# Seven products for a quarter of the query and key projection in a two-layer trunk kernel

## The chip, the cores and the metric

The kernel runs on one core of one Trainium2 chip. The metric is the device time of one execution in microseconds (us); lower is better. Before the change it is 1020.06 us, the median of three runs (1020.04 to 1020.19). One further execution was profiled; its trace is what the views below are read from.

## The reference

The model has two layers over 256 tokens of width 2048, all in float32. The first mixes HGRN2 and RG-LRU heads; after it and after the second layer, a gate built from the hidden state scales a per-layer embedding. The second layer is an mLSTM. The change touches its first projection, which gives queries and keys, and the hand-over to it from the gate of the first layer:

```python
    h = h + mix
    pl = rmsnorm(p[i].astype(h.dtype) @ ple_w[i], ple_norm[i])
    h = h + jax.nn.sigmoid(h @ ple_gate_w[i]) * pl       # end of layer 0: the gate "g0"
    hn = rmsnorm(h, o_norm[j])                           # layer 1 begins
    u = hn @ o_w_in[j]                                   # 2048 x 8208
    qk = u[..., 0:2 * C_QK]                              # 2048 columns: queries, keys
    v = u[..., o0:o0 + C_WIDTH]                          # 2048 columns: values ("ov")
    qk = jax.nn.silu(causal_conv(qk, c_conv_w[j], c_conv_b[j]))
```

## The kernel before

**Tiling.** A projection of 2048 columns is cut into four chunks of 512 columns. Its contraction of 2048 is cut into four quarters (`kq` 0 to 3) of 512. The 256 tokens are two halves (`hf`) of 128. The stationary side of a matmul is a 128x128 block of features by tokens, the moving side 128x512 of weights. Float32 exactness is kept by splitting both sides into a high and a low part and adding three matmuls (high-high, high-low, low-high). So one quarter of one chunk is 2 halves x 4 blocks x 3 = 24 matmuls (`quarter_tok`, lines 200 to 215, or `plain`, 241 to 247).

**Weights.** A quarter of a chunk comes as two tiles of 128x1024 (512 KB). SyncE (SP) issues the load into one of five `raw` tiles (line 134); ScalarE (ACT) copies the high part into one of four `whi` tiles (137), VectorE (DVE) subtracts for the low part in one of four `wlo` (138). The same split for tiles that are loaded by hand is `split_weights` (217 to 223).

**Seven products.** `seven` (288 to 397) computes two chunks at once for a pair of token halves. In the quarters listed in `kqs` it splits the contraction in two, which makes a 2x2 by 2x2 block product, and does that with seven block products of six matmuls each in place of eight. The weight tiles are X, Y, Z and W; sums of them are formed in place, by DVE (`add`) or by an accumulating transfer that POOL issues (`add_loaded`, line 314, when `acc` is true). The features enter in four combinations that `combos` (249 to 286) makes from the features of the quarter and stores, high and low, in two tiles `q4`. The products go to PSUM banks A, F, B (`mm`) and E (`mx`), partial results to two half tiles `b5` and `g`. The remaining quarters are plain. The order is a string: `a` and `b` are plain quarters of the first and second chunk, the digits are products, `.` lets waiting side work advance, `A` and `F` hand out a result.

**Side work.** Generators wait in named lanes; `pump()` advances each lane by one step, in the middle of a quarter and at `.`. Tile allocation and waits are made by the framework, which also orders the instructions of each engine by priority: the splits of weights come early (`high_priority`, lines 136, 220).

**Around the change.** `two_and_seven` (187 to 198) runs the gate g0: two plain chunks, then `seven` on the other two. `ple_gate` (610 to 626) applies tanh and the embedding, turns each finished chunk into features by a DVE transpose and a hop through device memory that POOL issues (`to_features`, `across`, lines 562 to 588 and 683 to 692), and stores them, scaled and split, as `acth` in twelve `ahl` tiles (lines 142 to 153). Two steps of `acth` are a quarter. `gate_sums` (1148 to 1156) reads the weight tile `wg` for 32 small matmuls.

Queries and keys (1226 to 1241) ran as `chunks`: `project_two` does chunks 0 and 1 in the order (0,0) (0,1) (1,0) (1,1) (0,2) (1,2) (0,3) (1,3) of (chunk, quarter), then chunks 2 and 3 follow whole. Each finished chunk goes through `features` (1196 to 1224): transpose, hop, convolution, SiLU. The lane "combos" (1228 to 1233) made the combinations of quarter 0 ten steps into this stage, in `h` tiles, for the value projection that comes next (`value_halves`, 1377 to 1384).

Of the kernel before, what the change touches and what calls it, by code (L numbers as in the profile page):

```python
# [19 lines left out]
P = 128  # L20
# [5 lines left out]
ORDERS = {1: "a5a6.2aA7b.4F.bb", 2: "a5.2aA64.7F.bb"}  # L26
LATE = "a526.a7b4aAF.bb"
# [18 lines left out]
def trunk(ctx: ExitStack, tc: tile.TileContext, a, out):  # L46
# [116 lines left out]
    def project_tok(w, j, act, before=None, begun=None):  # L163

        ps = begun or [pm.tile([P, 512], F32, name="mm", tag="mm") for _ in range(2)]
        for kq in range(1 if begun else 0, 4):
            if before is not None:
                before(kq)
            quarter_tok(w, j, kq, act, ps)
        return ps  # L170
# [77 lines left out]

    def combos(act, kq, qs, pool, tag, bufs=None, offset=0):
# [14 lines left out]
        def keep(c, names):  # L264
            q = pool.tile([P, 1024], F32R, name="q4", tag=tag, bufs=bufs)
            with tc.high_priority(offset=offset):
                s.copy(q[:, 0:512], c)
                v.tensor_tensor(out=q[:, 512:1024], in0=c, in1=q[:, 0:512].bitcast(F32), op=ALU.subtract)
            for n, name in enumerate(names):
                qs[name, kq] = [[q[:, i * 512 + n * T + k * P:i * 512 + n * T + (k + 1) * P] for k in range(2)]  # L270
                                for i in range(2)]
# [16 lines left out]
    def seven(w, j, act, qs, kqs, room, part, home=None, order=None, acc=None, before=None, third=None):  # L288
# [38 lines left out]
        def combo(n):  # L327
            return [[t for kq in kqs for t in qs[n, kq][x]] for x in range(2)]
# [5 lines left out]
        A, F, B = (pm.tile([P, 512], F32, name="mm", tag="mm") for _ in range(3))  # L334
# [12 lines left out]
        if third is not None:  # L347
            plain(w, j + 2, kqs[0], act, third, (True, True))
        Y = load(room, 1, 1)
        product(E, combo(4), split(Y), home is None)  # L350
        W = X
        if not acc:
            W = load(ring, 1, 0)
            add(Y, W)
            add(W, X)
        did = set()
        for op in order or ORDERS[len(kqs)]:
            if op in "ab":
# [251 lines left out]
    def ple_gate(hq, parts, pls, rp, hss, gain, lane, more):  # L610

        nxt = {}
# [13 lines left out]
        return nxt  # L626
# [513 lines left out]
    wt = e0.tile([P, KT, 32], F32, name="wg")  # L1140
# [17 lines left out]
    acth = ple_gate(hq, two_and_seven(a["g0"], act, ready(act, "fe"), (e0, "q4", 2), in_e0), pls, rp0, hss0, "on", "fg", gate_sums)  # L1158
# [34 lines left out]
    with tc.tile_pool(name="m1", bufs=2) as m1:  # L1193
# [32 lines left out]
        qs = {}  # L1226

        def early():
            for _ in range(10):
                yield  # L1230
            yield from combos(acth, 0, qs, hp, "h")

        start("combos", early())
        for j, ps in enumerate(chunks(a["oqk"], 4, acth, ready(acth, "fg"))):
            if j == 0:
                drain("norm")
            t = m1.tile([P, 2, 512], F32, name="tqk", tag="vt", bufs=6)
            for hf in range(2):
                s.activation(t[:, hf], ps[hf], AF.Copy, scale=norm["rt"][:, hf:hf + 1])
            start(f"qk{j}", features(t, j))  # L1240
            step(f"qk{j}")
# [7 lines left out]
        li, xf, ab, Bc, Mx = (t8(n) for n in ("li", "xf", "ab", "Bc", "Mx"))  # L1249
        lf = xf  # L1250
# [126 lines left out]
        def value_halves():  # L1377
# [3 lines left out]
            drain("combos", "spill")  # L1381
# [153 lines left out]
        def gates():  # L1535
# [3 lines left out]
            for hf, ps in enumerate(project_tok(a["g1"], 2, act, None, third)):  # L1539
                yield 2, hf, ps  # L1540
# [196 lines left out]
```

## Time and profile before

| what | value |
|---|---|
| median of 3 runs | 1020.06 us |
| profiled execution, its own time | 1020.23 us |
| its span, first to last instruction | 1018.4 us |
| mean granted TensorE clock | 0.998 |
| matmuls / VectorE / ScalarE instructions | 5158 / 1234 / 949 |
| gate g0, `seven` part | 429.4 to 473.1 us |
| queries and keys | from 472.9 us |

How to read it: PE is the matmul part of TensorE and PEld its loading of stationary blocks, which overlaps; DVE is VectorE, ACT ScalarE, POOL GpSimd, SP SyncE. L235 is line 235 of the kernel before. A matmul group `mm<-whi,ahl` writes a PSUM tile `mm` from `whi` and `ahl`. In the views, "idle before" is the time in which an engine had nothing to do, with what ended it behind the arrow.

### The profile page before, as it was taken

How to read it: one execution, taken by the hardware profiler on the slowest of the kernel's cores; microseconds unless marked ns; L12 is line 12 of the kernel's file. 1: busy time of each engine (PE TensorE's matmuls, PEld its weight loads, DVE VectorE, ACT ScalarE, POOL GpSimd, SP SyncE). 2: the span in 40 equal slices, each digit the busy share in tenths (PEclk: the TensorE clock that was granted, in tenths of full speed). 3: DMA queues.
4: the chain of work that ended last, by engine and by line, in shares of the span. 5: the costliest groups of instructions: out<-in, count | busy, mean ns of one | idle time of the engine just before them, and what ended most of it. 6: DMA issues, size and time to landing. Idle time of an engine off the chain costs nothing.

```text
span 1018.4 us, 14515 instructions
## 1 busy us (share of the span) xinstructions
PE 1009.4 (99%) x5158; PEld 838.1 (82%) x5158; DVE 842.8 (83%) x1234; ACT 661.4 (65%) x949; POOL 101.3 (10%) x182
## 2 busy tenths in 40 slices
PE   9999999999999999999999999999999999999996
PEld 8888888888888888888888888888888888888886
DVE  7858969969687887898669997888889997999794
ACT  7675554686875554666557877776676777466562
POOL 0111101011111112021011100000011110102000
PEclk9999999999999999999999999999999999999999
DMA  9987756567778799487798757567879889696852
GB/s 364 330 233 240 225 177 197 166 204 225 251 235 305 238 315 291 155 284 249 258 337 250 228 166 227 166 208 201 256 193 283 233 249 356 181 288 217 279 186 83
DMA packets 69816, 242.66 MB, mean 238 GB/s; under 512 B 9040, under 2 KB 10448, under 8 KB 69744
## 3 DMA queue, kind: packets, MB, share of 16 engines
q1 hardware_dynamic: 56016, 198.08, 58.7%
q0 software_dynamic: 13296, 43.13, 16.1%
q8 instruction: 40, 0.66, 0.3%
q10 hardware_dynamic: 432, 0.52, 0.1%
q14 instruction: 32, 0.26, 0.1%
HBM read 221.78 MB, written 19.92 MB: 237 GB/s over the span
## 4 chain that ended last, share of the span: by engine, by line
PE 99%; ACT 0%; DMA 0%; issue 0%; DVE 0%; ACTq 0%; POOLq 0%
PE mm L235 29%; PE mm L211 14%; PE mm L212 14%; PE mm L213 14%; PE mx L235 8%; PE mx L211 3%; PE mx L212 3%; PE mx L213 3%; PE mm L517 1%; PE nu L1349 1%; PE mx L517 1%; PE mm L1562 1%; PE mm L1561 1%; PE mm L1563 1%; PE st L213 1%; PE st L235 1%
## 5 line engine op out<-in xcount | busy, mean ns | idle before, releaser
L137 ACT CAST whi<-raw 128x1024 fp32r<-128x1024 f32 (+1 forms) x309 | 322.6, 1047 | 211.3 <-PE mm L213 95.2
L138 DVE TENSOR_TENSOR wlo<-raw,whi 128x1024 fp32r<-128x1024 f32 (+1 forms) x309 | 371.6, 1213 | 104.0 <-ACT whi L137 97.8
L211 PE MATMUL mm<-whi,ahl 128*128 128x512 f32 x640 | 250.5, 392 | 0.0
L212 PE MATMUL mm<-wlo,ahl 128*128 128x512 f32 x640 | 249.4, 390 | 0.0
L213 PE MATMUL mm<-whi,ahl 128*128 128x512 f32 x640 | 249.3, 389 | 0.0
L235 PE MATMUL mm<-whi,ahl 128*128 128x512 f32 x720 | 231.8, 390 | 0.0
L235 PEld LDWEIGHTS mm<-whi,ahl 128*128 128x128 f32 x720 | 135.2, 188 | 27.9
L211 PEld LDWEIGHTS mm<-whi,ahl 128*128 128x128 f32 x640 | 120.2, 188 | 25.5 <-issue 0.4
L213 PEld LDWEIGHTS mm<-whi,ahl 128*128 128x128 f32 x640 | 120.2, 188 | 25.1
L235 PE MATMUL mm<-wlo,ahl 128*128 128x512 f32 x360 | 140.5, 390 | 0.0
L212 PEld LDWEIGHTS mm<-wlo,ahl 128*128 128x128 f32 x640 | 120.2, 188 | 24.3
L222 DVE TENSOR_TENSOR wlo<-ch,whi 128x1024 fp32r<-128x1024 f32 x67 | 81.1, 1221 | 12.5 <-ACT whi L221 11.1
L221 ACT CAST whi<-ch 128x1024 fp32r<-128x1024 f32 x67 | 70.1, 1050 | 26.8 <-PE mm L235 13.8
L235 PEld LDWEIGHTS mm<-wlo,ahl 128*128 128x128 f32 x360 | 67.6, 188 | 14.1 <-DVE wlo L222 0.3
L235 PE MATMUL mx<-whi,ahl 128*128 128x512 f32 x192 | 63.3, 390 | 0.0
L212 PE MATMUL mx<-wlo,ahl 128*128 128x512 f32 x128 | 49.8, 389 | 0.0
L213 PE MATMUL mx<-whi,ahl 128*128 128x512 f32 x128 | 49.8, 389 | 0.0
L211 PE MATMUL mx<-whi,ahl 128*128 128x512 f32 x128 | 49.8, 389 | 0.0
L235 PE MATMUL mm<-whi,q 128*128 128x512 f32 x144 | 49.1, 391 | 0.0
L235 PEld LDWEIGHTS mx<-whi,ahl 128*128 128x128 f32 x192 | 36.1, 188 | 7.9 <-ACT xr L575 0.4
L235 PE MATMUL mx<-wlo,ahl 128*128 128x512 f32 x96 | 37.4, 390 | 0.0
L235 PEld LDWEIGHTS mm<-whi,q 128*128 128x128 f32 x144 | 27.0, 188 | 5.7
(389 smaller groups left out, 1318.5 us busy)
## 6 DMA issues: line engine op xcount, KB each, us to landing
raw<-in_ew_dram SPq DMA_DIRECT2D x64, 512.0 KB, 5.2
raw<-in_g_dram SPq DMA_DIRECT2D x60, 512.0 KB, 4.5
raw<-in_oqk_dram SPq DMA_DIRECT2D x32, 512.0 KB, 5.5
raw<-in_eo_dram SPq DMA_DIRECT2D x30, 512.0 KB, 5.1
raw<-in_oo_dram SPq DMA_DIRECT2D x30, 512.0 KB, 6.4
raw<-in_ov_dram SPq DMA_DIRECT2D x29, 512.0 KB, 4.2
raw<-in_oog_dram SPq DMA_DIRECT2D x24, 512.0 KB, 4.1
raw<-in_oz_dram SPq DMA_DIRECT2D x20, 512.0 KB, 5.1
```

What stands on the lines that cost most here:

```text
L137: last["act"] = s.copy(h, r).ins
L138: last["dve"] = v.tensor_tensor(out=l, in0=r, in1=h.bitcast(F32), op=ALU.subtract).ins
L211: te.matmul(ps[hf], xh, wh, start=(k == 0), stop=False, skip_group_check=True)
L212: te.matmul(ps[hf], xh, wl, start=False, stop=False, skip_group_check=True)
L213: last["pe"] = te.matmul(ps[hf], xl, wh, start=False, stop=(k == KT - 1), skip_group_check=True).ins
L221: last["act"] = s.copy(hi, r).ins
L222: last["dve"] = v.tensor_tensor(out=lo, in0=r, in1=hi.bitcast(F32), op=ALU.subtract).ins
L235: last["pe"] = te.matmul(o, x, y, start=(first and k + i == 0), stop=(end and k == n - 1 and i == 2), skip_group_check=True).ins
L517: last["pe"] = te.matmul(ps[hf][:, o:o + w_], tokens(pact[x], k, hf), (hi, lo)[y][:, k * 512 + o:k * 512 + o + w_], start=(n == mine[0]), ...
L1349: te.matmul(ps[:, 0:n], x[:, i, o:o + P], y[:, b, i], start=(b == 0 and x is sh and y is vh), stop=(b == hf and y is vl))
L1561: te.matmul(o, xh, wh, start=(k == 0), stop=False)
L1562: te.matmul(o, xh, wl, start=False, stop=False)
```

## The change

Chunks 0 and 1 of the queries and keys go through `seven`, with quarter 0 in seven products. Chunk 2 gets its quarters 0 and 1 as `c` and `d` directly behind the first product, in two `mx` banks; its quarters 2 and 3 and chunk 3 follow plainly. What was the fixed second step of `seven` (load Y, product with E, W) becomes a letter `3` of the order, so the other orders begin with `3`.

The combinations of quarter 0 are made earlier, in the lane "early" that starts within g0 (`begin`), in two `ahl` tiles; eight steps later `moved` copies them to `h` tiles for the values. X and Y of the new `seven` also take `ahl` tiles; its half tiles `b5` and `g` are one `vt` tile. The tile `wg` moves into a pool of its own that stays open, so that nothing later is laid over it. `Mx` shares the tile of `ab`. `acth` is handed into `ple_gate` from outside, so that "early" can see it.

```diff
-ORDERS = {1: "a5a6.2aA7b.4F.bb", 2: "a5.2aA64.7F.bb"}
-LATE = "a526.a7b4aAF.bb"
+ORDERS = {1: "3a5a6.2aA7b.4F.bb", 2: "3a5.2aA64.7F.bb"}
+LATE = "c3a526.a7b4aAF.bb"
...
-    def project_tok(w, j, act, before=None, begun=None):
+    def project_tok(w, j, act, before=None, begun=None, done=0):
...
-        for kq in range(1 if begun else 0, 4):
+        for kq in range(done, 4):
...
+    def moved(qs, kq, pool, tag):
+
+        for q, names in qs["tiles", kq]:
+            t = pool.tile([P, 1024], F32R, name="q4", tag=tag)
+            s.copy(t, q.bitcast(F32))
+            known(qs, kq, t, names)
+            yield
...
-        if third is not None:
-            plain(w, j + 2, kqs[0], act, third, (True, True))
-        Y = load(room, 1, 1)
-        product(E, combo(4), split(Y), home is None)
-        W = X
-        if not acc:
-            W = load(ring, 1, 0)
-            add(Y, W)
-            add(W, X)
         did = set()
         for op in order or ORDERS[len(kqs)]:
-            if op in "ab":
+            if op in "cd":
+                plain(w, j + 2, "cd".index(op), act, third, (op == "c",) * 2)
+            elif op == "3":
+                Y = load(room, 1, 1)
+                product(E, combo(4), split(Y), home is None)
+                W = X
+                if not acc:
+                    W = load(ring, 1, 0)
+                    add(Y, W)
+                    add(W, X)
+            elif op in "ab":
...
-                pe0.append(l0.enter_context(tc.tile_pool(name="e0", bufs=1)))
+                wg = ctx.enter_context(tc.tile_pool(name="wgp", bufs=1))
+                pe0.extend((l0.enter_context(tc.tile_pool(name="e0", bufs=1)), wg))
...
+    def early():
+        yield from combos(acth, 0, qs, ap, "ahl")
+        for _ in range(8):
+            yield
+        yield from moved(qs, 0, hp, "h")
...
-        def early():
-            for _ in range(10):
-                yield
-            yield from combos(acth, 0, qs, hp, "h")
-
-        start("combos", early())
-        for j, ps in enumerate(chunks(a["oqk"], 4, acth, ready(acth, "fg"))):
+        def in_ap():
+            return ap.tile([P, 1024], F32, name="ch", tag="ahl")
+
+        def queries_keys():
+            third = [px.tile([P, 512], F32, name="mx", tag="mx") for _ in range(2)]
+            pr = pieces(m1.tile([P, 1024], F32, name="pr", tag="vt", bufs=6))
+            while (4, 0) not in qs:
+                step("early")
+            yield from seven(a["oqk"], 0, acth, qs, (0,), in_ap, pr, order="cd3a526.a7b4aAF.bb", acc=True,
+                             before=ready(acth, "fg"), third=third)
+            for j, begun in ((2, third), (3, None)):
+                for hf, ps in enumerate(project_tok(a["oqk"], j, acth, None, begun, 2 if begun else 0)):
+                    yield j, hf, ps
...
-        li, xf, ab, Bc, Mx = (t8(n) for n in ("li", "xf", "ab", "Bc", "Mx"))
-        lf = xf
+        li, xf, ab, Bc = (t8(n) for n in ("li", "xf", "ab", "Bc"))
+        lf, Mx = xf, ab
...
-            drain("combos", "spill")
+            drain("early", "spill")
```

More of the change, by code (lines that the diff above doesn't have):

```diff
@@ L247, in plain, with known @@
                 pump()
+    def moved(qs, kq, pool, tag):
[4 more added lines that the diff above has]
+            yield
+    def known(qs, kq, q, names):
+        for n, name in enumerate(names):
+            qs[name, kq] = [[q[:, i * 512 + n * T + k * P:i * 512 + n * T + (k + 1) * P] for k in range(2)]
+                            for i in range(2)]
     def combos(act, kq, qs, pool, tag, bufs=None, offset=0):
@@ L268, in keep @@
                 v.tensor_tensor(out=q[:, 512:1024], in0=c, in1=q[:, 0:512].bitcast(F32), op=ALU.subtract)
-            for n, name in enumerate(names):
-                qs[name, kq] = [[q[:, i * 512 + n * T + k * P:i * 512 + n * T + (k + 1) * P] for k in range(2)]
-                                for i in range(2)]
+            known(qs, kq, q, names)
+            qs.setdefault(("tiles", kq), []).append((q, names))
         while 2 * kq + 1 not in act:
@@ L286, in combos, with seven @@
         yield
-    def seven(w, j, act, qs, kqs, room, part, home=None, order=None, acc=None, before=None, third=None):
+    def seven(w, j, act, qs, kqs, room, part, home=None, order=None, acc=None, before=None, third=None, first=pm):
         def src(b, side, kq):
@@ L333, in seven @@
         E = px.tile([P, 512], F32, name="mx", tag="mx")
-        A, F, B = (pm.tile([P, 512], F32, name="mm", tag="mm") for _ in range(3))
+        A, F, B = (p.tile([P, 512], F32, name=n, tag=n)
+                   for p, n in ((first, "mm" if first is pm else "mx"), (pm, "mm"), (pm, "mm")))
         b5, g = part(), part()
@@ L608, in out_proj, with ple_gate @@
         return act
-    def ple_gate(hq, parts, pls, rp, hss, gain, lane, more):
-        nxt = {}
+    def ple_gate(hq, parts, pls, rp, hss, gain, lane, more, nxt):
         for c, hf, src in parts:
@@ L625, in ple_gate @@
                 squared(hq[c][:, hf], hss[:, c, hf:hf + 1])
-        return nxt
     def small(n, name, rows=P):
@@ L1139, in trunk @@
     sy.dma_start(out=gr, in_=a["ogf"])
-    wt = e0.tile([P, KT, 32], F32, name="wg")
+    wt = pe0[1].tile([P, KT, 32], F32, name="wg")
     gp.memset(wt, 0.0)
@@ L1156, in gate_sums @@
         held5.clear()
-    acth = ple_gate(hq, two_and_seven(a["g0"], act, ready(act, "fe"), (e0, "q4", 2), in_e0), pls, rp0, hss0, "on", "fg", gate_sums)
+    acth, qs = {}, {}
+    def early():
[3 more added lines that the diff above has]
+        yield from moved(qs, 0, hp, "h")
+    ple_gate(hq, two_and_seven(a["g0"], act, ready(act, "fe"), (e0, "q4", 2), in_e0, None, lambda: start("early", early())),
+             pls, rp0, hss0, "on", "fg", gate_sums, acth)
     away = []
@@ L1224, in features @@
                 yield
-        qs = {}
-        def early():
-            for _ in range(10):
-                yield
-            yield from combos(acth, 0, qs, hp, "h")
-        start("combos", early())
-        for j, ps in enumerate(chunks(a["oqk"], 4, acth, ready(acth, "fg"))):
-            if j == 0:
-                drain("norm")
[L1237 to L1241, printed above, removed]
+        def in_ap():
[10 more added lines that the diff above has]
+                    yield j, hf, ps
+        for j, hf, src in queries_keys():
+            if (j, hf) == (0, 0):
+                drain("norm")
+            if hf == 0:
+                t = m1.tile([P, 2, 512], F32, name="tqk", tag="vt", bufs=6)
+            s.activation(t[:, hf], src, AF.Copy, scale=norm["rt"][:, hf:hf + 1])
+            if hf:
+                start(f"qk{j}", features(t, j))
+                step(f"qk{j}")
         VW = 258
@@ L1538, in gates @@
             yield from seven(a["g1"], 0, act, qs1, (0,), *in_m1(), order=LATE, before=before, third=third)
-            for hf, ps in enumerate(project_tok(a["g1"], 2, act, None, third)):
+            for hf, ps in enumerate(project_tok(a["g1"], 2, act, None, third, 1)):
                 yield 2, hf, ps
```

## The prediction, made before the changed kernel was run

> **What bounds the kernel now.** I read the page first (busy time, then the chain that ended last), then the chain in order of time, where each run of matmuls carries its time and count, and then busy time by stage around the edit.
>
> ```profile
> PE 1009.4 (99%) x5158; PEld 838.1 (82%) x5158; DVE 842.8 (83%) x1234; ACT 661.4 (65%) x949; POOL 101.3 (10%) x182
> PE 99%; ACT 0%; DMA 0%; issue 0%; DVE 0%; ACTq 0%; POOLq 0%
> ```
>
> TensorE (PE) is busy and is the chain, both to 99%. So time goes only where matmuls go, and comes only where PE would have to wait. The next view prices a matmul. In the chain in order of time the columns are start, length, what, count:
>
> ```profile
> 343.69 1.36 PE mm L235 x6
> 345.06 1.36 PE mx L235 x6
> 346.42 21.76 PE mm L235 x96
> 429.38 1.36 PE mm L235 x6
> 430.73 1.40 PE mx L235 x6
> 432.13 21.96 PE mm L235 x96
> 460.92 1.00 PE st L1154 x16
> 508.43 1.00 PE st L1154 x16
> 750.78 24.48 PE mm L235 x108
> 882.86 1.40 PE mx L235 x6
> 932.10 16.40 PE mm L235 x72
> ```
>
> A dense stream gives 24.48 / 108 = 0.2267 us a matmul, so one product of six is 1.36 us and one quarter (24 matmuls in `quarter_tok` or `plain`) 5.44 us. The same rows price the helper `seven` at work: in the first gate of the even layer's output (343.69 on) it runs with no loss at all, in `g0` (429.38 on) with 0.04 + 0.20 us lost, in the last gate with the `LATE` order with 0.04 + 0.08 us (16.40 against 72 x 0.2267 = 16.32).
>
> Then the stage of the edit. The columns are the stretch, PE, PEld, DVE, ACT and POOL busy, granted clock, DMA share, GB/s:
>
> ```profile
> 429.40:473.10 43.70, 43.70 (x203) 35.29 (x203) 38.38 (x44) 31.50 (x49) 6.47 (x12) 1.00 0.73 239
> 473.10:483.00 9.90, 9.90 (x45) 8.19 (x44) 9.55 (x24) 5.15 (x10) 2.33 (x5) 1.00 0.99 313
> 483.00:494.00 11.00, 11.00 (x51) 9.09 (x50) 7.70 (x14) 7.09 (x11) 2.19 (x4) 1.00 0.83 287
> 473.10:560.20 87.10, 87.10 (x396) 71.42 (x395) 68.14 (x108) 54.01 (x80) 12.90 (x26) 1.00 0.88 285
> ```
>
> PE has no hole in any of them. VectorE (DVE) has some 20% free over queries and keys as a whole, but 0.35 us of 9.9 in the stretch where the new products begin, and DMA is at 0.99 there. That corner is what could hurt.
>
> **The change, part by part.** *The products.* Chunks 0 and 1 with quarter 0 were eight products (two token halves, two column chunks, two halves of the contraction), 48 matmuls. `seven` does them in seven, 42. Six matmuls go: 6 x 0.2267 = 1.36 us. Nothing else on PE changes in number: chunk 2's quarters 0 and 1 only move ahead (`c`, `d`), and `project_tok` then starts at quarter 2. The other uses of `seven` issue what they did: `3` at the head of an order, or behind `c`, is the code that stood before the loop. Expected matmuls: 5158 - 6 = 5152.
>
> The Trainium skill's page "TensorE: Matmul & The Clock Gate", section "Back-to-back issue gap", gives about 131 ns for a sustained matmul of 512 columns; that would make the gain 0.8 us and the time some 0.6 us later than mine. The trace does not agree, with 227 ns in the densest row above, so I keep 1.36.
>
> *What PE gives back.* The three rows of `seven` bound it: 0 to 0.24 us, and 0.12 us under the order most like the new one. I take 0.15. Net: -1.2 us.
>
> *VectorE and ScalarE work.* Rows for the kinds of work, from the groups of the two stages (the last numbers are busy us, mean ns | idle before):
>
> ```profile
> L138 DVE TENSOR_TENSOR wlo<-raw,whi 128x1024 fp32r<-128x1024 f32 x32 | 38.9, 1223 | 14.6 <-ACT whi L137 13.5
> L253 DVE TENSOR_TENSOR xr<-ahl 128x512 f32<-128x512 f32 x2 | 1.3, 686 | 0.0
> L258 DVE TENSOR_TENSOR qc<-xr 128x256 f32<-128x256 f32 x2 | 0.8, 423 | 0.0
> L268 DVE TENSOR_TENSOR q<-qc,q 128x512 fp32r<-128x512 f32 x2 | 1.4, 688 | 0.7 <-ACT q L267 0.7
> L310 DVE TENSOR_TENSOR ch<-ch,raw 128x1024 f32<-128x1024 f32 x1 | 1.2, 1219 | 0.0
> L318 DVE TENSOR_TENSOR pr<-mx,pr 128x512 f32<-128x512 f32 x1 | 0.7, 683 | 0.0
> L137 ACT CAST whi<-raw 128x1024 fp32r<-128x1024 f32 x14 | 14.6, 1046 | 5.1 <-PE mm L235 5.1
> L322 ACT COPY pr<-mm 128x512 f32<-128x512 f32 x2 | 1.2, 587 | 0.7 <-PE mm L235 0.7
> ```
>
> Seven splits replace four: +3 x 1.22 on DVE, +3 x 1.05 on ACT. Two sums of weight tiles (X with Y, X with Z): +2 x 1.22 DVE. Three corrections of partial sums (`soon`): +3 x 0.68 DVE. Four bank copies (F, B, b5, g): +4 x 0.59 ACT. `moved` copies two tiles: +2 x 1.05 ACT. Together DVE +8.1, ACT +7.6 us, where the queries-and-keys stage has 87.1 - 68.1 = 19.0 and 33.1 free: off the path as a whole. The seven combined stationary pieces are not new: `combos` (DVE 2 x 0.69 + 4 x 0.42 + 2 x 0.69 = 4.4 us) only moves, from the middle of the stage to behind chunk 0's features, at the end of `g0`. `moved` (two ACT copies into an `h` tile) is what the value projection reads later in its place.
>
> *Where it could bite.* Up to the third product in a row (`5`, `2`, `6`) the new order takes five products and three quarters: 5 x 1.36 + 3 x 5.44 = 23.1 us, the same as 4.25 quarters of before. In these, DVE prepares 5 + 6 = 11 splits for 8.5, and two sums: +2.5 x 1.22 + 2.4 = 5.5 us. The two stretches 473.10 to 494.00 had 20.9 - 17.25 = 3.65 us free, so about 1.9 us must slip. What may slip is read from the timelines (start, length, engine, what):
>
> ```profile
> 472.91 0.39 PE L211 MATMUL mm<-whi,ahl 128*128 128x512 f32 x1
> 457.00 1.30 DVE L152 TENSOR_TENSOR ahl<-xr,ahl 128x512 fp32r<-128x512 f32 x2
> 461.02 2.57 DVE L138 TENSOR_TENSOR wlo<-raw,whi 128x1024 fp32r<-128x1024 f32 x2 [2.72 <-ACT whi L137]
> 488.32 0.69 DVE L152 TENSOR_TENSOR ahl<-xr,ahl 128x512 fp32r<-128x512 f32 x1
> 498.73 0.69 DVE L152 TENSOR_TENSOR ahl<-xr,ahl 128x512 fp32r<-128x512 f32 x1 [0.37 <-ACT ahl L151]
> ```
>
> Queries and keys begin at 472.91. Quarter 2's features are ready at 489.01, quarter 3's at 499.42. Before, PE asked for them after 4 and 6 quarters, at 494.7 and 505.6. In the new order it asks at 472.91 + 23.1 = 496.0 and, an `a` quarter, a `b` quarter and the products `4` and `7` later (5.44 + 5.44 + 2.72), at 509.6. Margins grow from 5.7 to 7.0 and from 6.1 to 10.2 us, which is what the two quarters of the third chunk buy. A slip of 1.9 us, even with all of `combos` on top (6.3 us), still fits. `combos` itself starts after 458.3, where DVE idles 2.72 us anyway, and is first read by the product `3` at 472.91 + 1.36 + 10.88 = 485.1. I cost all of this at nothing; were the margin gone, up to the whole 6.3 us would be PE's.
>
> *Transfers.* SP issues three weight tiles (X, Y, Z) in place of four, POOL two accumulating ones:
>
> ```profile
> raw<-in_oqk_dram SPq DMA_DIRECT2D x32, 512.0 KB, 5.5
> ch<-in_ov_dram POOLq DMA_DIRECT2D x2, 512.0 KB, 6.6
> 484.15 2.19 POOL L689 DMA_DIRECT2D r<-dfg  x4 [4.74 <-PE mm L213]
> 515.68 0.56 POOL L686 DMA_DIRECT2D dqk<-w  x1 [29.35 <-DVE w L1201]
> L314 POOL DMA_DIRECT2D ch<-in_ov_dram x2: 855/894/932, 601.4 to 612.9; - x2
> ```
>
> The first accumulation waits for X's split, before 474.3, and lands 6.6 us later; it is read at 492. If it is queued ahead of chunk 3's hop (r<-dfg), that hop moves by 0.9 us out of 10.2. The second waits for X + Y, about 492, and is read by `7` at 508.3; the next thing on POOL is the first hop of the queries at 515.7. One extra 512 KB at 313 GB/s is 1.7 us of DMA in a stage with a share of 0.88: nothing, or 1.7 us on a hop with the margins above.
>
> *Room.* X and Y now live in `ahl`, twelve tiles: eight features, two combined pieces, X and Y fill it exactly. When X is wanted (its load 5.5 and split 2.3 us before 472.9, so by 465) four features of chunks 0 and 1 are in, and of the eight old ones those of quarter 0 and 1 have been read for the last time when the products and the first `b` quarter of `g0` are done, just before the gate sums at 460.92. 12 - 4 - 4 = 4 are free then, two for the combined pieces, two for X and Y. It fits, 4 us early. Taking the tile `wg` out of the pool that `m1` overlays removes a wait: its last reader is the second group of gate sums at 508.43, and the new tile `pr` is first written after `5`, at 493.3. `Mx` in the place of `ab` adds none: line 1274 reads `ab` on the engine that writes `Mx` at line 1277. In PSUM, A takes the bank that `g0` gave up first, and the third chunk the two `mx` banks of `g0`'s plain chunk 1, both long read.
>
> **The sum.** -1.36 + 0.15 = -1.2 us. The profiled execution took 1020.23 us with a span of 1018.4, so 1.8 us lie around it; the median 1020.06 is 0.17 less. I subtract from the median: 1018.9 us. A difference of 0.2% (2.0 us, to 1018.0 or 1022.1) is about what can be told from no change here, so the forecast lies inside it: same.
>
> **The rivals.** *Given back.* The three products in a row need 3 splits and 2 sums, 6.1 us of DVE for 4.1 us of PE. If the four split tiles do not hold enough in stock, PE waits 2.0 us: 1020.06 - 1.36 + 2.0 = 1020.7. For it: 0.35 us of slack in 9.9. Against: `LATE` has the same row of three at DVE loads like this and lost 0.12. 18%. Here too belongs that the matmuls do not go (5158 stays, 1020.1), which the code rules out nearly: 3%.
>
> *Slower: X has no tile.* If a tile for X comes free only with the last `b` quarter of `g0`, at 472.9, the first product waits for the load and the split, 5.5 + 1.05 + 1.22 = 7.8 us: 1020.06 - 1.36 + 7.8 = 1026.5. It decides from the point at which X's load is issued later than 465; each us after that is one us of PE, and after 468.5 the kernel is slower by over 0.2%. Against it is the count of tiles above; for it, that the pool is filled to the last one and that a load which waits for its tile holds up the weight loads of `c` and `d` behind it in SP's queue. 7%.
>
> *Faster by more.* The busiest stretch of DVE, at the end of the stage, loses `combos` and gets chunk 1's convolutions later. If PE waited there, that would come on top, 0.7 us or more: 1018.0. But the chain shows no wait there. 4%.
>
> **How the numbers follow.** Forecast 68% (1018.5 to 1019.6), given back or no removal 21%, slower 7%, faster 4%. Same is 68 + 21 = 0.89, faster 0.04, slower 0.07. The range takes the forecast's bounds (losses 0 to 0.24 us, and a few tenths of reordering elsewhere) and the given-back case: 1018.2 to 1020.8.
>
> **What would show it.** PE with 5152 matmuls and still 99%; no L211 on PE between the end of `g0` and chunk 2's third quarter; the queries-and-keys stage shorter by 1.2 us; DVE nearly full from 473 to 496; the last L152 before 496.0 and 509.6. A hole on PE right at 472.9 would show the slower rival, holes at `2` or `6` (493 to 496) the given-back one. I am wrong if matmul counts fall by 6 and the span does not follow, or if it falls by over 2 us.

## The result, and the profile after

| | before | after |
|---|---|---|
| median of 5 runs, same chip | 1020.19 us | 1024.06 us |
| lowest to highest | 1020.04 to 1020.36 | 1023.81 to 1025.43 |
| profiled execution / its span | 1020.23 / 1018.4 | 1025.43 / 1023.6 |

The ratio of the times is 1.0040 with a 95% interval of 1.0026 to 1.0055: the changed kernel is slower by 3.9 us, where 1.2 us less was forecast, and it lies outside the range.

From the page of the changed kernel, the busy time and the shares of the chain:

```profile
PE 1010.9 (99%) x5152; PEld 836.8 (82%) x5152; DVE 849.8 (83%) x1242; ACT 667.3 (65%) x958; POOL 103.4 (10%) x184
PE 90%; DVE 6%; DMA 2%; ACT 2%; issue 1%; ACTq 0%; POOL 0%; DVEq 0%; POOLq 0%
```

The six matmuls went (5152), yet TensorE's share of the chain fell from 99% to 90%: DVE, a transfer and ACT are on it now. That share is far more than was lost, for the chain leaves TensorE long before each wait while TensorE still works (from 559.00 to 613.50 us PE is busy for all 54.50 us, though the chain runs mostly over DVE). Where time was lost, TensorE's own timeline shows (start, length, what, and in brackets the idle time before it with what ended it):

```profile
496.40 0.39 PE L235 MATMUL mm<-wlo,ahl 128*128 128x512 f32 x1
498.42 0.73 PE L235 MATMUL mm<-whi,ahl 128*128 128x512 f32 x2 [1.63 <-DVE ahl L152]
...
503.33 0.39 PE L235 MATMUL mm<-whi,ahl 128*128 128x512 f32 x1
504.62 0.50 PE L235 MATMUL mm<-whi,q 128*128 128x512 f32 x1 [0.90 <-ACT whi L221]
505.88 0.72 PE L235 MATMUL mm<-wlo,q 128*128 128x512 f32 x1 [0.76 <-DVE wlo L222]
506.40 1.06 PE L235 MATMUL mm<-whi,q 128*128 128x512 f32 x2
507.25 0.63 PE L235 MATMUL mm<-wlo,q 128*128 128x512 f32 x1
```

A row's loss is the time to the next row's start, less 0.2267 us for each of its matmuls. The first two rows lose 2.02 - 0.23 = 1.79 us: quarter 2 of the first chunk waits for its features (`ahl`, line 152). The next two waits, 1.06 and 1.03 us, are product 7 (`mm<-whi,q`), which waits for the two halves of the split of Y. From 505.88 on nothing is waited for, but the matmuls come 0.43 us apart. The stage view says why (stretch, PE, PEld, DVE, ACT, POOL busy, granted clock, DMA share, GB/s):

```profile
472.90:496.20 23.30, 23.30 (x104) 19.02 (x103) 21.58 (x40) 16.46 (x25) 6.83 (x11) 1.00 0.94 291
501.25:506.25 5.00, 3.35 (x13) 2.26 (x13) 1.65 (x2) 2.73 (x3) 0.00 (x0) 0.97 0.73 290
506.25:509.25 3.00, 3.00 (x8) 2.35 (x8) 2.75 (x4) 3.00 (x4) 0.00 (x0) 0.50 0.44 141
508.00:511.50 3.50, 3.50 (x14) 2.74 (x14) 3.25 (x5) 3.50 (x7) 0.00 (x0) 0.80 0.88 283
```

The granted clock is 0.50 there; the means of the stretches around it (0.97 over 5 us is 0.3 us at half, 0.80 over 3.5 us is 1.4) put it from about 505.95 to 509.4. That costs 1.70 us more, summed over the rows from 505.88 to 509.63. With 0.40 us that the `seven` of the values loses at 613.51 (before: nothing), and several of about 0.1, the losses from 460 to 660 us are 6.57 us, against 0.23 before. So 1018.4 - 1.36 + 6.57 - 0.23 = 1023.4, where the span is 1023.6. The loss is placed.

**Why quarter 2's features are late.** They had been ready at 489.01. ScalarE's timeline around their scaling (`xr`, line 590):

```profile
486.71 1.06 ACT L221 CAST whi<-raw 128x1024 fp32r<-128x1024 f32 x1 [0.30 <-PE mx L235]
490.83 1.05 ACT L221 CAST whi<-ch 128x1024 fp32r<-128x1024 f32 x1 [3.07 <-DVE rcr L421]
491.79 0.90 ACT L590 ACTIVATE xr<-r,prm 128x256 f32<-128x256 f32 x2
```

ScalarE sat idle for 3.07 us ahead of the split for product 6, which had to wait, and the features stood behind it in ScalarE's own order. The row names VectorE's `rcr`, but X + Y had been ready since 489.2, and in `e_lag6` below the same split starts at the same moment behind TensorE: most likely it waits until TensorE has read one of the four `whi` tiles for the last time. No run isolates that. VectorE then did the second half (`ahl`) at 497.68 and 498.71, so they were ready at 499.40, 10.4 us later than before, and asked for at 496.6.

**Why product 7's split is late.** Y gets W added by the accumulating transfer of line 327. POOL's timeline, and then the chain from there:

```profile
483.93 0.56 POOL L699 DMA_DIRECT2D dfg<-w  x1 [7.56 <-DVE hss L456]
491.79 2.18 POOL L702 DMA_DIRECT2D r<-dfg  x4 [7.29 <-issue]
493.96 0.96 POOL L327 DMA_DIRECT2D ch<-in_oqk_dram  x1
```

```profile
493.96 9.48 DMA ch<-in_oqk_dram
503.52 1.05 ACT whi L221
504.60 1.24 DVE wlo L222
505.88 2.43 PE mm L235 x5
```

X + Y (`ch<-ch`, line 323) ran at 487.95 and was over at 489.2, but on POOL the transfer stands behind chunk 3's hop, whose reads (`r<-dfg`) could go out only at 491.79, when the write ahead of them had landed. The transfer then took 9.48 us, and the split 2.3 more. Product 7 stands right behind the `a` of quarter 2, so TensorE would have asked at 501.5.

### The profile page after: what moved, and what is told of

Read it like the earlier page. It is cut to its first block, busy times and chain, and to the rows that moved or that the text cites. A ratio compares the mean times of both kernels' runs of the same rounds, so it can differ in the third digit from the quotient of the medians.

```text
span 1023.6 us, 14515 instructions
## 1 busy us (share of the span) xinstructions
PE 1010.9 (99%) x5152; PEld 836.8 (82%) x5152; DVE 849.8 (83%) x1242; ACT 667.3 (65%) x958; POOL 103.4 (10%) x184
## 4 chain that ended last, share of the span: by engine, by line
PE 90%; DVE 6%; DMA 2%; ACT 2%; issue 1%; ACTq 0%; POOL 0%; DVEq 0%; POOLq 0%
PE mm L235 31%; PE mm L211 11%; PE mm L212 11%; PE mm L213 11%; PE mx L235 9%; PE mx L213 2%; PE mx L212 2%; PE mx L211 2%; DVE wlo L138 2%; DVE qk L1241 1%; DMA ch<-in_oqk_dram 1%; PE nu L1379 1%; PE mm L532 1%; DMA raw<-in_pw_dram 1%; PE mm L1591 1%
## 5 line engine op out<-in xcount | busy, mean ns | idle before, releaser
L138 DVE TENSOR_TENSOR wlo<-raw,whi 128x1024 fp32r<-128x1024 f32 (+1 forms) x305 | 366.1, 1212 | 99.6 <-ACT whi L137 94.1
L235 PE MATMUL mm<-whi,ahl 128*128 128x512 f32 x804 | 259.1, 390 | 1.9 <-DVE ahl L152 1.6
L211 PE MATMUL mm<-whi,ahl 128*128 128x512 f32 x576 | 225.3, 392 | 0.0
L212 PE MATMUL mm<-wlo,ahl 128*128 128x512 f32 x576 | 224.6, 390 | 0.1
L213 PE MATMUL mm<-whi,ahl 128*128 128x512 f32 x576 | 224.2, 389 | 0.0
L235 PEld LDWEIGHTS mm<-whi,ahl 128*128 128x128 f32 x804 | 150.9, 188 | 34.4 <-DVE ahl L152 2.1
L235 PE MATMUL mm<-wlo,ahl 128*128 128x512 f32 x402 | 156.7, 390 | 0.0
L213 PEld LDWEIGHTS mm<-whi,ahl 128*128 128x128 f32 x576 | 108.2, 188 | 22.5
L211 PEld LDWEIGHTS mm<-whi,ahl 128*128 128x128 f32 x576 | 108.1, 188 | 22.5
L222 DVE TENSOR_TENSOR wlo<-ch,whi 128x1024 fp32r<-128x1024 f32 x73 | 88.4, 1220 | 18.4 <-ACT whi L221 17.0
L221 ACT CAST whi<-ch 128x1024 fp32r<-128x1024 f32 x73 | 76.2, 1050 | 34.7 <-PE mm L235 13.3
L235 PE MATMUL mx<-whi,ahl 128*128 128x512 f32 x248 | 81.6, 392 | 0.0
L235 PEld LDWEIGHTS mx<-whi,ahl 128*128 128x128 f32 x248 | 47.0, 190 | 10.3 <-ACT whi L137 0.4
L235 PE MATMUL mm<-whi,q 128*128 128x512 f32 x156 | 54.2, 396 | 0.9 <-ACT whi L221 0.9
L235 PE MATMUL mx<-wlo,ahl 128*128 128x512 f32 x124 | 48.5, 391 | 0.0
L211 PE MATMUL mx<-whi,ahl 128*128 128x512 f32 x112 | 43.6, 389 | 0.0
L212 PE MATMUL mx<-wlo,ahl 128*128 128x512 f32 x112 | 43.6, 389 | 0.0
L213 PE MATMUL mx<-whi,ahl 128*128 128x512 f32 x112 | 43.6, 389 | 0.0
```

The costliest lines, as they stand in the source:

```text
L138: last["dve"] = v.tensor_tensor(out=l, in0=r, in1=h.bitcast(F32), op=ALU.subtract).ins
L211: te.matmul(ps[hf], xh, wh, start=(k == 0), stop=False, skip_group_check=True)
L212: te.matmul(ps[hf], xh, wl, start=False, stop=False, skip_group_check=True)
L213: last["pe"] = te.matmul(ps[hf], xl, wh, start=False, stop=(k == KT - 1), skip_group_check=True).ins
L221: last["act"] = s.copy(hi, r).ins
L222: last["dve"] = v.tensor_tensor(out=lo, in0=r, in1=hi.bitcast(F32), op=ALU.subtract).ins
```

## The experiments

Eighteen kernels ran, each in four to twelve timed executions beside the kernel before on the same chip. "Losses" are TensorE's, from 460 to 660 us, by the rule above, in the profiled execution.

| kernel | median us | ratio to before (95%) | span | losses |
|---|---|---|---|---|
| e_side | 1020.59 | 1.0003 (0.9994 to 1.0011) | 1017.9 | 0.23 |
| e_pair23 | 1029.71 | 1.0093 (1.0079 to 1.0108) | 1027.2 | 9.32 |
| e_lag6 | 1028.03 | 1.0079 (1.0062 to 1.0095) | 1025.6 | 6.66 |
| e_noacc | 1024.60 | 1.0038 (1.0026 to 1.0050) | 1022.2 | 4.79 |
| e_half | 1027.05 | 1.0068 (1.0055 to 1.0081) | 1024.9 | 8.06 |
| e_lag6_half | 1023.77 | 1.0030 (1.0019 to 1.0042) | 1022.1 | 3.17 |
| e_lag6_c3 | 1027.72 | 1.0075 (1.0063 to 1.0088) | 1028.7 | 5.84 |
| e_lag6_half_c3 | 1027.37 | 1.0068 (1.0051 to 1.0085) | 1023.4 | 4.59 |
| e_7late | 1027.83 | 1.0075 (1.0061 to 1.0089) | 1025.4 | 8.27 |
| e_ba47 | 1020.25 | 1.0001 (0.9992 to 1.0009) | 1017.8 | 0.88 |
| e_fg6_7late | 1020.18 | 0.9996 (0.9987 to 1.0005) | 1017.8 | 0.88 |
| e_fg6_ba47 | 1020.21 | 0.9996 (0.9988 to 1.0005) | 1017.4 | 0.85 |
| e_fg6_parts | 1022.81 | 1.0026 (1.0015 to 1.0037) | 1021.2 | 3.79 |
| e_parts | 1025.91 | 1.0056 (1.0042 to 1.0070) | 1022.2 | 5.42 |
| e_fg6_half_4 | 1022.24 | 1.0021 (1.0011 to 1.0031) | 1020.9 | 4.00 |
| e_half_parts | 1022.38 | 1.0027 (1.0016 to 1.0037) | 1020.4 | 3.79 |
| e_fg6_end | 1021.67 | 1.0020 (1.0011 to 1.0029) | 1019.9 | 2.77 |
| e_fg6_half_end | 1022.99 | 1.0030 (1.0018 to 1.0042) | 1021.2 | 4.37 |

The five medians of the kernel before were 1020.37 (rows 1 to 4), 1020.26 (next four), 1020.03 (next four), 1020.29 (next four) and 1020.17. My theory was that the late features and the late accumulation are the whole loss; the rivals were the side edits, the place of the seven products, and a VectorE and ScalarE so full that every wait closed opens another.

### What the side edits cost

`e_side` keeps all side edits (early combinations, `moved`, `wg`, `Mx`), but runs queries and keys plainly:

```diff
-            yield from seven(a["oqk"], 0, acth, qs, (0,), in_ap, pr, order="cd3a526.a7b4aAF.bb", acc=True,
...
+            for j, ps in enumerate(chunks(a["oqk"], 4, acth, ready(acth, "fg"))):
```

> All the side edits stay (combinations made early in g0's tail, copied later, wg in its own pool, Mx on ab, letters 3/c/d), but queries and keys run as plain chunks as before. Theory (two waits of the new products): nothing is lost, 1020.1 us within 0.5. Rival (the side edits themselves load VectorE and ScalarE at the hand-over): 1022 us or more. Rival (the seven products overload VectorE wherever they stand): also 1020.1.

Ratio 1.0003, span 1017.9: they cost nothing. That part of the prediction holds, and the loss belongs to the seven products.

### Another place for the seven products

`e_pair23` runs chunks 0 and 1 plainly and puts the seven products on chunks 2 and 3, where all features are long ready:

```diff
+            for j, ps in enumerate(project_two(a["oqk"], acth, ready(acth, "fg"))):
...
+            for b, hf, src in seven(a["oqk"], 2, acth, qs, (0,), in_ap, pr, acc=True):
```

> Same six matmuls saved, but on chunks 2 and 3 of queries and keys, behind the two plain chunks, so that the products stand away from the hand-over from g0. Theory (the place: features of quarter 2 and an accumulation are late at the hand-over): no waits, 1020.1 - 1.36 + 0.2 = 1018.9 us. Rival (the method: 8 us more VectorE work in this stage, wherever): 1022 us or more. Rival (side edits): 1022 or more.

It was the slowest of all, by another wait. TensorE's timeline:

```profile
608.30 0.39 PE L235 MATMUL mm<-whi,ahl 128*128 128x512 f32 x1
613.68 1.09 PE L1358 MATMUL mx<-qhl,khl 128*128 128x256 f32 x3 [4.99 <-ACT khl L1351]
```

The first attention scores wait 4.99 us for keys. The pair finishes late, both chunks together, and its convolutions have no projection behind them to hide under. So the expectation, which looked only at the start of the stage, was wrong.

### One wait at a time

`e_lag6` gives the features' hop six steps in place of seven before they are written out:

```diff
-        yield from across(w, r, f"d{name}{c}", 7 if c == 2 else 6)
+        yield from across(w, r, f"d{name}{c}", 6)
```

> One number changed in the changed kernel: chunk 2's features are issued one step of side work earlier (lag 6 in place of 7), which puts them ahead of the splits for products 5, 2 and 6 on ScalarE. Theory: the hole of 1.9 us before quarter 2's first matmuls goes, 1024.1 - 1.9 = 1022.2 us; the one at product 7 stays unless the accumulation also comes earlier. Rival (VectorE is simply full): the hole moves elsewhere, 1024 us.

The wait at quarter 2 is gone, and the time is worse. TensorE's timeline:

```profile
501.25 0.39 PE L235 MATMUL mm<-whi,ahl 128*128 128x512 f32 x1
504.42 0.49 PE L235 MATMUL mm<-whi,q 128*128 128x512 f32 x1 [2.79 <-ACT whi L221]
505.68 0.63 PE L235 MATMUL mm<-wlo,q 128*128 128x512 f32 x1 [0.77 <-DVE wlo L222]
```

TensorE comes to product 7 earlier (501.48 against 503.56) and goes on at 505.68, where the changed kernel did at 505.88. The accumulation lands when it did (503.24, before 503.44), and what the first wait gave back the second took. ScalarE's timeline shows what the edit moved: the scaling now stands ahead of the split for product 6, and that split still starts where it did.

```profile
485.04 0.91 ACT L590 ACTIVATE xr<-r,prm 128x256 f32<-128x256 f32 x2
490.79 1.06 ACT L221 CAST whi<-ch 128x1024 fp32r<-128x1024 f32 x1 [0.96 <-PE mm L235]
```

The edit also lost 2.0 us at 942 to 950 us, where layer 1's features now come at another step. `e_noacc` and `e_half` attack the accumulation instead; the first loads W by SP and adds on VectorE both times, the second only for Y:

```diff
-            yield from seven(a["oqk"], 0, acth, qs, (0,), in_ap, pr, order="cd3a526.a7b4aAF.bb", acc=True,
+            yield from seven(a["oqk"], 0, acth, qs, (0,), in_ap, pr, order="cd3a526.a7b4aAF.bb", acc=False,
```

```diff
-                if acc:
+                if acc and third is not None:
+                    add(Y, load(ring, 1, 0))
+                elif acc:
                     add_loaded(Y)
```

> W is loaded once by SyncE and added twice by VectorE in place of two accumulating transfers of GpSimd. Theory: product 7 no longer waits for a transfer (-2.1 us) while the features of quarter 2 are still late: about 1022 us. Rival (VectorE is full): two more sums of 1.22 us make it worse, 1025 to 1026 us.

> One thing is undone: the second accumulating transfer of queries and keys (Y += W). W's block comes by SP's own load and VectorE adds it. The features of chunk 2 stay as late as in the changed kernel. Theory (two separate late chains, each with its own hole): the hole before product 7 (2.1 us) is gone, the one before quarter 2 (1.9 us) stays, the half clock after it is seen in fewer executions, so about 1021.8 us. Rival (one common lateness: chunk 3's features are late as well, and whatever comes next waits for them): the hole moves to the quarter of chunk 3 behind product 7, and the time stays near 1024.

In both, product 7 waits for nothing. In `e_noacc` quarter 2 still loses 1.9 us, and a new 1.2 us stands at 514, because ScalarE's next splits queue behind chunk 3's features, which wait for their hop:

```profile
510.54 1.31 ACT L590 ACTIVATE xr<-r,prm 128x256 f32<-128x256 f32 x3 [3.04 <-DMA r<-dfg]
```

In `e_half` quarter 2's loss grew from 1.8 to 4.5 us, and 0.9 us came at the first product; neither theory had that, for both took the features' ready time as given. Each wait undone alone gave 1024.6 to 1028.0, never less than the change.

### Both waits, and chunk 3's hop

`e_lag6_half` joins the two. `e_lag6_c3` keeps the accumulation, and lets chunk 3's tanh, gate and transposes go ahead of the splits, so that its hop leaves POOL earlier; `e_lag6_half_c3` has all three.

```diff
-            th = tp.tile([P, 512], F32, name="th", tag="th")
+            with tc.high_priority(offset=450 if c == 3 else 0):
+                th = tp.tile([P, 512], F32, name="th", tag="th")
...
```

> Both holes are attacked at once: chunk 2's features are written out one step earlier (lag 6 in place of 7) and the second accumulation is a load and a VectorE add. Theory (two separate chains): both holes go, 1.9 + 2.1 us less than the changed kernel, about 1020.0 us, within 0.5 us of the kernel before. Rival (one common lateness): chunk 3's hop is late anyway, its quarter behind product 7 waits, 1022 us or more.

> Chunk 2's features one step earlier as before; the second accumulation stays on POOL, but chunk 3's tanh, gate and transposes stand ahead of the splits for products 5, 2 and 6 on ScalarE and VectorE (a priority), so that chunk 3's hop on POOL, behind which the accumulation is queued, is issued about 4 us earlier. Theory (the accumulation is late because the hop ahead of it on POOL waits for VectorE): it lands about 4 us earlier, near 499.5 us, product 7's hole of 2.9 us is gone, about 1020.5 us against 1028.0 with the lag alone. Rival (the transfer is late by itself, whatever POOL does): still near 503.5 us, 1024 or more; other rival (the splits that now stand behind are late instead): holes of 1 to 3 us at products 5 to 6, 1022 or more.

> All three: chunk 2's features one step earlier, the second accumulation as a load and an add, chunk 3's gate and transposes ahead of the splits. Theory: no hole of over 0.5 us between 473 and 560 us, about 1019.3 us, near the forecast of the prediction. Rival (VectorE and ScalarE hold too much work in these 40 us in any order): one or two holes of over 1 us elsewhere in the stage, 1021 us or more.

`e_lag6_half` is 1023.77, not 1020.0: 0.95 us at quarter 2, 1.12 us at the first product (its block X landed later), and the 2.0 us of the lag at 942. With chunk 3 ahead, product 7 waits for nothing, but the third rival came true, on TensorE's timeline of `e_lag6_c3`:

```profile
478.45 0.62 PE L235 MATMUL mx<-whi,ahl 128*128 128x512 f32 x2
481.67 0.80 PE L235 MATMUL mx<-wlo,ahl 128*128 128x512 f32 x1 [2.59 <-DVE wlo L138]
482.26 1.05 PE L235 MATMUL mx<-whi,ahl 128*128 128x512 f32 x2
```

The splits that were pushed back are late, 2.77 us, and `e_lag6_half_c3` loses the same there. So in this place chunk 3's chain costs as much as it was to save. The accumulation did not come earlier either: X + Y itself moved to 496.00, the transfer was issued at 497.79 and landed at 504.03, where in `e_lag6` it was issued at 494.05 and landed at 503.24. Product 7 does not wait only because TensorE comes to it as late as 508.89. So that an earlier hop brings the accumulation earlier is not shown.

### Asking later

If what is late can't come earlier, it can be asked for later. In `e_7late` product 7 stands behind `b` and `4`, which is where the prediction had read it; in `e_ba47` the second chunk's quarter 1, whose features are old, also stands ahead of quarter 2; `e_fg6_7late` and `e_fg6_ba47` add the lag of six for these features alone.

```diff
-            yield from seven(a["oqk"], 0, acth, qs, (0,), in_ap, pr, order="cd3a526.a7b4aAF.bb", acc=True,
+            yield from seven(a["oqk"], 0, acth, qs, (0,), in_ap, pr, order="cd3a526.ab47aAF.bb", acc=True,
```

(`ba47`: "cd3a526.ba47aAF.bb"), and for `fg6`:

```diff
-        yield from across(w, r, f"d{name}{c}", 7 if c == 2 else 6)
+        yield from across(w, r, f"d{name}{c}", 6 if name == "fg" else 7 if c == 2 else 6)
```

In these four the second chunk's quarter goes into bank B before product 7 is read out of it, so the partial sum that is read contains it: the same instructions, but another sum than the reference's.

> Only the place of product 7 changes: it stands behind the second chunk's plain quarter and product 4 (where the prediction had read it), 24 matmuls or 5.4 us later, and everything else of the changed kernel stays. Theory (the accumulation lands at about 503.4 us whatever TensorE does, and its split is over at 505.9 us): product 7 is then asked for at about 507 us and waits for nothing, the 2.1 us are gone and with them the half clock behind them, the 1.9 us at quarter 2 stay: about 1021.9 us. Rival (VectorE and ScalarE have too much queued in this stage, so any hole that is closed opens behind it): a hole of over 1 us at the next quarter, 1023.5 us or more.

> As before with product 7 late, and the second chunk's plain quarter 1 (which needs no late feature) stands ahead of the first chunk's quarter 2: chunk 2's features are asked for 2.7 us later, at about 499.1 us where they were ready at 499.4. Theory (two late chains, each with a fixed ready time): both holes are under 0.5 us, about 1020.0 us, between 1019.2 and 1020.6. Rival (the split for the quarter that now comes first stands ahead of chunk 2's features on ScalarE, and makes them later by as much): a hole of 1 to 2 us at quarter 2 stays, 1021 to 1022 us.

> Product 7 late, and lag 6 in place of 7 for the features that queries and keys read alone (the runs with lag 6 everywhere also lost 1.8 us at 944 us, far behind this stage, which this one should not). Theory: no hole over 0.5 us at quarter 2 or product 7, about 1020.0 us. Rival (loss moves on): first product or chunk 3's quarter waits over 1 us, 1022 us or more.

> All three: lag 6 for these features, the second chunk's quarter 1 first, product 7 late. Theory: both chains have 2 us or more to spare, the stage runs without a hole of over 0.5 us, about 1019.3 us, 0.9 under the kernel before. Rival (too much on ScalarE and VectorE in any order): still a hole of over 1 us somewhere between 470 and 560 us, 1021 us or more.

With both asked for later, or one later and the other earlier, the stage has no wait. The chain of `e_fg6_7late` in order of time:

```profile
470.46 4.08 PE mm L235 x18
474.54 12.24 PE mx L235 x54
486.78 14.96 PE mm L235 x66
501.74 2.72 PE mx L235 x12
504.46 8.16 PE mm L235 x36
```

All TensorE, each row at 0.2267 us a matmul, from 470 to 512.6. The late transfers are as late as ever: POOL issues the accumulation at 494.07 and the split of Y begins at 502.49, but nobody asks for it. All three are level with the kernel before.

`e_7late` alone was 1027.83, the rival's time, though not at the rival's place. Product 7 no longer waits, but quarter 2's loss grew to 4.48 us. VectorE's timeline:

```profile
497.41 2.36 DVE L138 TENSOR_TENSOR wlo<-raw,whi 128x1024 fp32r<-128x1024 f32 x2
500.07 1.22 DVE L138 TENSOR_TENSOR wlo<-raw,whi 128x1024 fp32r<-128x1024 f32 x1
501.69 1.29 DVE L152 TENSOR_TENSOR ahl<-xr,ahl 128x512 fp32r<-128x512 f32 x2
```

More splits of the coming quarters now stand ahead of the features on VectorE (`ahl` at 501.69, before 497.68). The recorded order of each engine changes with the order of the products, and in none of these runs did one wait move alone.

### With the reference's sum

Six more orders read bank B out in the right place. `e` and `f` are the two halves of the second chunk's quarter 1, for banks E and B, so that E's half can go ahead of product 7:

```diff
+            elif op == "e":
+                kq = rows[1].pop(0)
+                before(kq)
+                held = load_weights(w[4 * (j + 1) + kq])
+                product(E, stationary(act, (2 * kq, 2 * kq + 1), 0), held)
+                pump()
+            elif op == "f":
+                product(B, stationary(act, (2 * kq, 2 * kq + 1), 1), held)
```

The order is "cd3a526.4ae7faAF.bb" in `e_parts` (lag 7), `e_fg6_parts` and `e_half_parts` (lag 6 for these features, load and add), "cd3a526.4a7baAF.bb" in `e_fg6_half_4`, and "cd3a526.ae47afAF.bb" in `e_fg6_end` and `e_fg6_half_end`.

> The sum of the reference is kept: product 4 goes ahead of the first chunk's quarter 2, and the second chunk's quarter 1 is cut in two: its half for bank E ahead of product 7, its half for bank B behind it. Product 7 is asked for 18 matmuls or 4.1 us later than in the changed kernel, quarter 2 one product or 1.4 us later, and chunk 2's features come one step earlier (lag 6 for these alone). Theory (two late readies and nothing else): no hole over 0.5 us, span 1017.4 to 1018.0 us, a median within 0.5 us of the kernel before. Rival (the other order saved the time, not the closed waits): a hole of 1 us or more at quarter 2, product 7 or the next quarter, 1022 us or more.

> The same order as the run before it, lag 7 as in the changed kernel: chunk 2's features late, asked for 1.4 us later. Theory (each late ready has its own price, and a hole at quarter 2 makes what stands behind it on ScalarE and VectorE late too): a hole of 0.5 to 4.5 us at quarter 2, none at product 7, 1021 to 1026 us. Rival (product 7's wait is the only cause): about 1020 us.

> The accumulation is done by a load and a VectorE add in place of being asked for later; product 4 ahead of quarter 2, lag 6 for these features alone. Theory: no wait at quarter 2 or product 7, about 1020 us, and 1 us more if the first product waits for its block at 473 us, as in two runs with the load in place of the accumulation. Rival (the add makes VectorE late): a hole of over 1 us in 495 to 515 us, 1022 us or more.

> All cures at once with the reference's sum: load and add, product 7 late by 4.1 us, quarter 2 by 1.4 us, lag 6 for these features. Theory: 1019.5 to 1020.5 us, and 1 us more if the first product waits at 473 us. Rival: over 1022 us through a new hole.

`e_parts`, 1025.91, lies 3.1 us over `e_fg6_parts`, which differs only in the lag: product 7's wait is not the only cause. But none came back to 1020. Two new waits explain it. Product 4, put ahead of quarter 2, needs X + Z, which is only then added and split (0.7 to 1.8 us at 495 to 499). And the B half right behind product 7 must wait until VectorE has read bank B out, on TensorE's timeline of `e_fg6_parts`:

```profile
509.06 0.39 PE L235 MATMUL mm<-whi,q 128*128 128x512 f32 x1
510.23 0.50 PE L235 MATMUL mm<-whi,ahl 128*128 128x512 f32 x1 [0.78 <-DVE pr L331]
```

The last two put both right: 4 behind E's half, and the first chunk's last quarter between product 7 and B's half. In these two that half multiplies by the last quarter's features in place of its own, which the `a` ahead of it needs anyway.

> The reference's sum is kept. Lag 6 for these features; behind quarter 2 come the second chunk's half quarter for bank E, product 4, product 7, the first chunk's last quarter, and only then the half quarter for bank B, so that VectorE has 5.4 us for reading B out. Theory (the waits are the whole cause): no hole over 0.5 us from 474 to 560 us, a span of 1017.4 to 1018.0 us and a median within 0.5 us of the kernel before, or 1 us more if the first product waits at 473 us. Rival (some wait always opens in this stage when the sum is kept): 1022 us or more.

> The same with the second accumulation as a load and a VectorE add. Theory: the same time as the run before it within 0.5 us, for with product 7 late enough the accumulation is off the path. Rival (the transfer on POOL still delays chunk 3's features): 1 us or more faster than the run before it.

1021.67, the nearest of those with a read-out in the right place: 0.48 us at the first product, 0.98 us at 508 (a split of the next quarter, late behind Y's), the rest small. With the load in place of the accumulation it is 1.3 us slower, not equal: 0.95 us are lost at quarter 2 and some 0.4 us more at the first product, against 0.4 us less at 508. That the load and its add make these late is likely, but was not taken apart. No order tried here that keeps the sum is level with the kernel before; whether there is one stays open.

## Why the prediction was wrong

**Right.** 5152 matmuls, no more and no less. The side edits at nothing (`e_side`). Room: X and Y were issued at 464.8 and 465.3, straight behind the load ahead of them, so "X has no tile" did not come; there was no wait at 472.9 in the changed kernel. But eight of the variants lost 0.4 to 1.1 us there, so X's landing had a margin of a fraction of a microsecond.

**The size of the gain.** In every kernel with the seven products the span follows: 1018.4 - 1.36 + losses - 0.23, and 2.0 us more where lag six stands everywhere (3.6 us in `e_lag6_c3`, with the half clock there). For `e_7late` that is 1025.1 (measured 1025.4), for `e_half` 1024.9 (1024.9), for `e_lag6_half` 1022.0 (1022.1), for `e_ba47` 1017.7 (1017.8). Two are off by over 0.7: `e_pair23` by 1.1, and `e_lag6_c3` by 2.5, of which over 2 us came before 462 us. So the spans fit 1.36 us saved, although the executions of the kernel before alone lie further apart than that (1019.62 to 1022.53 us beside `e_7late`). But 0.4 to 0.5 us are always given back in the values' `seven` at 607 to 615, in all seventeen kernels that have the new products on chunks 0 and 1, and in neither `e_side` nor the kernel before; what delays ScalarE's copy there (line 359) was not tried. The kernels with no other loss measure 0.9996 to 1.0001: even without the waits, a gain can't be told from no change.

**Step one that failed: "A slip of 1.9 us, even with all of `combos` on top (6.3 us), still fits."** The features slipped by 10.4 us. I had priced VectorE's work against its free time as if the late work could slip into any gap. VectorE was indeed not full (21.58 of 23.30 us from 472.90 to 496.20, above), and ScalarE was idle for 3.07 us right before the split ahead of the scaling. What set the time was the place in ScalarE's queue, behind a split that waited itself. Lag six, which only changes that place, brought the scaling from 491.79 to 485.04 and removed the wait (`e_lag6`); the rest of the slip came on VectorE, where the last part stood behind two more splits.

**Step two: "is read by `7` at 508.3".** I counted a `b` and a `4` ahead of 7; the string "a7b4a" has them behind it. The right sum is 496.0 + 5.44 = 501.4, as in the trace (501.5 without the waits).

**Step three: "the next thing on POOL is the first hop of the queries at 515.7".** I looked at what came after the accumulation on POOL and not at what stood ahead of it. I wrote of the first one that it might be queued ahead of chunk 3's hop; the second was queued behind it, and that hop itself had moved, because chunk 3's transposes came only at 482.34: VectorE did four splits ahead of chunk 3's gate and two more ahead of the transposes. With the issue at 493.96, even the 6.6 us that I had read and the split of 2.3 us give 502.9 against 501.4.

**No term for the clock.** After three waits within 9.5 us the clock was halved, 1.7 us more in the profiled execution. The other four of the changed kernel were 1.1 to 1.6 us faster, about that much, and their mean granted clocks were 0.997 to 0.999 against its 0.996. So its half clock is most likely not in the median, and what the median lost is mainly the waits.

**The rivals.** "Given back" had the kind right (a late split stalls TensorE), at the wrong place (product 7 and quarter 2, not the three products in a row) and with 2.0 us where 3.9 were lost in waits and 1.7 to the clock. The slower rival had the side right and the mechanism wrong.

The two late readies as the cause of the change's own loss are shown by the runs that close both and come back level; that they can be cured with the sum kept is not.

## What to carry to other kernels

Free time of an engine over a stage does not say that work can slip into it: find the instruction in the engine's own queue, and ask what stands ahead of it and whether that one waits. A change that asks for more splits moves every other chain that is queued on the same engines, and closing one wait may only uncover or lengthen the next; look at what is ready a few microseconds later before counting the gain. Read an order written as a string letter by letter, with a time at each letter, before using one of its times.

## What the runs showed of the hardware

The clock fell to half for short stretches after waits. In the profiled execution of the changed kernel, waits of 1.79, 1.06 and 1.03 us ended at 505.88, and the clock was 0.50 from then to about 509.4. In `e_7late` one wait of 4.48 us did it. It was not the same each time: at the same place in `e_lag6_half` and `e_lag6_c3` TensorE lost 1.15 and 0.67 us; in the first the matmuls ran on at full pace, in the second they took twice as long (0.63 us records):

```profile
945.30 0.74 PE L235 MATMUL mm<-whi,ahl 128*128 128x512 f32 x2 [0.99 <-DVE ahl L601]
945.87 0.39 PE L235 MATMUL mm<-wlo,ahl 128*128 128x512 f32 x1
946.77 0.74 PE L235 MATMUL mm<-whi,ahl 128*128 128x512 f32 x2 [0.51 <-DVE ahl L601]
947.35 0.40 PE L235 MATMUL mm<-wlo,ahl 128*128 128x512 f32 x1
```

```profile
950.28 0.73 PE L235 MATMUL mm<-whi,ahl 128*128 128x512 f32 x2 [0.99 <-DVE ahl L599]
950.85 0.39 PE L235 MATMUL mm<-wlo,ahl 128*128 128x512 f32 x1
951.75 0.74 PE L235 MATMUL mm<-whi,ahl 128*128 128x512 f32 x2 [0.51 <-DVE ahl L599]
...
953.47 0.63 PE L235 MATMUL mm<-wlo,ahl 128*128 128x512 f32 x1
```

The traces' records of the granted clock fix when it changes. In the changed kernel it is full from 4.23 to 505.99, half to 509.40 and full again to 1017.99: 501.76, 3.41 and 508.59 us, or 147, 1 and 149 times 3.413 us. In all twenty traces the stretches between two changes are whole multiples of that, so the clock changes on a fixed grid. Two steps of the grid in the changed kernel, of which only the second was followed by half clock (columns as in the stage view above):

```profile
495.75:499.16 3.41, 1.78 (x8) 1.19 (x7) 3.24 (x8) 1.73 (x4) 0.00 (x0) 1.00 1.02 232
502.57:505.99 3.42, 1.77 (x8) 0.91 (x7) 1.39 (x2) 2.47 (x3) 0.00 (x0) 1.00 0.69 280
```

From 200 to 1005 us of all traces, the five full-clock steps with PE busy for 0.41 to 1.32 us were each followed by half clock, of six with 1.63 to 1.92 us two were, and of those with 2 us or more none.

The Trainium skill's page "TensorE: Matmul & The Clock Gate", section "What's actually happening", gives a window of 3413 ns that runs free of the kernel, and a half clock after an idle one. The length and the halving agree with this case's stretch of 3.4 us, and a free window fits the grid. Its place does not explain the difference between `e_lag6_half` and `e_lag6_c3`, for in each run both waits lie whole within one step, with PE busy for 1.92 us of it; that stays open. That TensorE must be idle for a whole window the runs do not show, for here waits of 1.15 and 0.67 us with work between them were enough.

Of the two accumulating transfers of 512 KB in this stage the first took 6.61 us, as the prediction's row from the values (6.6), and the second 9.48 us; it was issued only when the hop ahead of it on POOL had gone out, 4.8 us after its input was ready.
